# Gate projections with tokens on partitions, turned through DRAM, and a planner with another load rate and finer keys

## The chip, the cores and the metric

The kernel runs on one core of one Trainium2 chip. The metric is the device time of one execution in microseconds; the median of three timed executions stands for the kernel. Beside these there is one profiled execution, from which every row of the trace comes.

## What is computed

A diffusion backbone of two layers over 256 latent tokens and 256 context tokens, 2048 channels, all in float32. Layer 0 runs two head groups side by side: neighbourhood attention (16 heads) and a bidirectional state-space scan (SSD, 8 groups). Each of them is multiplied by a SiLU gate that is projected from the same normalised input. Layer 1 is a gated short convolution. Cut to what the change touches:

```python
p = h @ w_in                                  # 256 x 2048 @ 2048 x 14400
ya = neighbourhood_attention(q, k, v, kc, vc, rpb)
ya = ya * jax.nn.silu(cols(p, COL_GATE_A, NA_WIDTH, 0))          # gate G, 2048 columns
yb = gated_group_rmsnorm(y_ssd + d * lat[0], cols(p, COL_Z, SSD_WIDTH, 0), ssm_norm_g)   # gate Z, 2048 columns
out = jnp.concatenate([ya, yb], axis=-1) @ w_out
x = x + gate[:, None] * out
```

## The kernel before

**Products in three parts.** Every large product is done in a reduced float32 form that TensorE streams at full rate. A weight chunk of 128 x 1024 values (512 KB) is loaded into one of five `raw` buffers (nine in the first phase, when four tiles of later use serve too), rounded by ScalarE into `wH` (L458), and the remainder is taken by VectorE into `wL` (L465). The input is held the same way as `hH` and `hL`. A product is the sum of three: hH wH + hL wH + hH wL. There are three pairs of wH and wL, and a chunk's low part gives the raw buffer back, which lets the next load be issued on SyncE's queue (L428).

**Two ways to lay a product.** `mm_ws` (L690) holds 128 columns of the weight as the stationary operand and streams the tokens: for a weight of 512 columns it needs, for each block of 128 input channels, 4 column blocks x 3 products. With the 256 latent tokens alone each matmul streams 256 columns. The result has channels on partitions. `mm_act` (L680) holds 128 tokens as the stationary operand and streams up to 512 weight columns: 2 token blocks x 3 products. The result has tokens on partitions. `proj(nc_, kind, ps, nxt)` (L731) runs one projection over the 16 blocks of input channels; its `kind` is a number of tokens for `mm_ws` and "act" for `mm_act`. In layer 0, Q, K and V use "act"; the SSD inputs B, C and X and the gates G and Z use `mm_ws`, because what uses them wants channels on partitions.

**The turn through DRAM.** Q and K come out with tokens on partitions and are needed the other way round. `kq_gen` (L1007) stores each normalised block of 128 tokens with its columns in a mixed order into a DRAM tensor, fetches it back with four DMAs, one for each group of 32 partitions (`fetch`, L241, issued on GpSimd's queue) into the tile D (`d_take`, L1003: one buffer, guarded by the flag `dfree`), and finishes with VectorE transposes of 32 x 32 blocks (`blocks`, L248). The heads take the same D tile for their probabilities (L1137 to L1152).

**The gates before.** `silu2_gen` (L1054) waits until the gate tile is free (`ok`: for G the four heads of the step before are done, for Z the two groups before), then takes tanh of half the projection from PSUM (ScalarE, L1059) and multiplies (th + 1) by the projection (VectorE, L1061) straight into the gate tile `gt` or `sz`, two PSUM banks for each gate. The banks are held until then.

**What sets the order.** The order of every engine's instructions is written out by the Python code before the kernel runs. A list of tasks (generators) yields what it needs next: an engine, tiles that must be ready, PSUM banks. `Plan` keeps an estimated time for each engine and each piece of a tile; `may` (L296) lets a task's next step be written when the plan says that its inputs are ready at about the time TensorE is at. Weight products are written in a fixed sequence, and between them `pump` writes the steps that are due: splits (`splits_try`, L491), attention heads (`head_gen`, L1074), SSD groups (`group_gen`, L1418), turns, and the matrix-vector products of later layers' modulation (`gemv_gen`, L840; its accumulation on VectorE is L857). A load costs its bytes divided by `RATE` in the plan, one load after another, with 1000 ns ahead of and behind it; a DMA that touches DRAM scratch has 3000 ns more. `keys` says which pieces of a tile count as one: 128 columns of an SBUF tile. The engines themselves run in order and wait on semaphores that follow from the real overlaps of tiles, whatever the plan thought.

**The sequence.** The first phase, about 170 us, runs in eight steps of 256 input channels: the products of the modulation weights (`ada_gen`, L746, which gives each step's A0 and S0), the modulated input of the step, and the partial products of K, V, Q and B. Then come G(0), dt, C, X and Z(0), then Q, K, G, V and the SSD inputs of the next quarter with Z, and so on; in the last quarter V and G come after Z, just before the out-projection. The out-projection, layer 1's in-projection and its out-projection are all "act".

Of the kernel before, what the change touches and what calls it, by code (L numbers as in the profile page):

```python
# [10 lines left out]
AF = mybir.ActivationFunctionType  # L11
ALU = mybir.AluOpType
AX = mybir.AxisListType

D = 2048
KB = 16
EPS = 1e-6
COL_Q, COL_G, COL_Z, COL_K, COL_V, COL_X = 0, 2048, 4096, 6144, 8192, 10240
# [19 lines left out]
class Plan:  # L38


    NAMES = {"PE": "PE", "DVE": "DVE", "Activation": "ACT", "Pool": "POOL", "SP": "SP"}
    RATE = 270.0

    def __init__(self):
        self.t = dict.fromkeys(("PE", "DVE", "ACT", "POOL", "SP"), 0.0)
# [4 lines left out]
    def keys(self, ap):  # L50
        a, n = ap.ap, ap.tensor.name
        if type(ap.tensor).__name__ == "Tile" and not n.startswith("dram"):
            lo = ap.offset % a[0][0] if a[0][0] else ap.offset
            hi = lo + sum(abs(s) * (c - 1) for s, c in a[1:])
            return [(n, u) for u in range(lo // 128, hi // 128 + 1)]
        if n.startswith("in_") or n.startswith("out_"):
            return []
        hi = ap.offset + sum(abs(s) * (c - 1) for s, c in a)
        return [(n, u) for u in range(ap.offset // 256, hi // 256 + 1)]
# [38 lines left out]
    def add(self, b):  # L98
# [10 lines left out]
        if op == "DMACopy":  # L109
# [4 lines left out]
            if e == "SP":  # L114
                self.dma = max(self.dma, s + 1000) + n / self.RATE
                done = free = self.dma + 1000
            else:
                done = free = max(self.dma, s + 1000) + n / self.RATE + 1500
            if any(a.tensor.name.startswith("dram") for a in ins + outs):
# [52 lines left out]
def kernel(ctx: ExitStack, tc, x, cx, ada_w, ada_b, w_in, w_out, sc_in, sc_out, rpb, small, const,  # L172
# [8 lines left out]
    w_in, w_out, sc_in, sc_out = (Laid(w, n) for w, n in ((w_in, "w_in"), (w_out, "w_out"), (sc_in, "sc_in"), (sc_out, "sc_out")))  # L181
    V, S, G, T, DMA = nc.vector, nc.scalar, nc.gpsimd, nc.tensor, nc.sync
    DMA2 = nc.scalar
    plan = Plan()
    E = plan.add

    def st(shape, tag, dt=F32, name=None):
        return sb.tile(list(shape), dt, tag=tag, name=name or tag, bufs=1)
# [12 lines left out]
    def drt(shape, name):  # L201
        return dr.tile(list(shape), F32, name="dram_" + name)
# [3 lines left out]
    free_t = [st([128, 512], f"tmp{k}") for k in range(NTMP)]  # L206
    free_h = [st([128, 256], f"half{k}") for k in range(NHALF)]
    free_b = [pj.tile([128, 512], F32, tag=f"bank{k}", name=f"bank{k}", bufs=1) for k in range(8)]
# [4 lines left out]
    KT, QT, Vt, gt = st([128, 4, 512], "KT"), st([128, 4, 256], "QT"), st([128, 4, 512], "Vt"), st([128, 4, 256], "gt")  # L213
    sz, xtm, yi = st([128, 4, 256], "sz"), st([128, 2, 512], "xtm"), st([128, 4, 256], "yi")
# [26 lines left out]
    def fetch(dst, src):  # L241

        n = src.shape[0] // 32
        for b in range(4):
            E(G.dma_start(dst[32 * b:32 * b + 32].rearrange("p t (a x) -> p (t a) x", a=4),
                             bass.AP(tensor=src.tensor, offset=src.offset + 128 * b, ap=[[512, 32], [32 * 512, n], [1, 128]])))

    def blocks(o, i):  # L248

        E(V.transpose(o.rearrange("p k (a j) -> p a k j", a=4), i.rearrange("p (a k j) -> p a k j", a=4, k=4)))  # L250

    urgent, side, back = [], [], []
    got = set()
# [4 lines left out]
    def spawn(q, gen, tmps=0, halves=0):  # L258
        q.append(Task(gen, tmps, halves))
# [120 lines left out]
    def banks(n):  # L380
        force(lambda: len(free_b) >= n)
        return [take(free_b) for _ in range(n)]
# [4 lines left out]
    def give(pool, *bs):  # L387
        pool.extend(bs)

    W_ = lambda eng, *aps, nb=0: (eng, aps, nb)  # L390
    when = lambda f: ("if", f, 0)
# [321 lines left out]
    def chunk(kb0, kind, ps, first, last, lhs=None):  # L713

        H, Lo = use()
        nb = H.shape[1]
        for j in range(nb):
            kb = kb0 + j
            aH, aL = (hH[kb], hL[kb]) if lhs is None else lhs(kb)
            f, l = first and j == 0, last and j == nb - 1  # L720
            if kind == "act":
                mm_act(ps, aH, aL, H[:, j], Lo[:, j], f, l)
            elif kind == "both":
                mm_both(ps, aH, H[:, j], Lo[:, j], f, l)
            else:
                mm_ws(ps, aH, aL, H[:, j], Lo[:, j], kind, f, l)
        used()
# [3 lines left out]
    def proj(nc_, kind, ps, nxt, leave=False):  # L731
        nb = 1024 // nc_
        for kb in range(0, KB, nb):
            if kb + 2 * nb >= KB:
                reserve[0] = nxt
            chunk(kb, kind, ps, kb == 0, kb + nb >= KB)
            if leave:
                free_rows[0] = kb + nb
        reserve[0] = 0
# [258 lines left out]
    attn = [0]  # L998

    kqd = drt([4, 768, 512], "kqd")  # L1000
    dfree = [True]

    def d_take(name):  # L1003
        dfree[0] = False
        return st([128, 2, 512], "PT0", name=name)
# [40 lines left out]
    def v_gen(a, ps):  # L1046
# [4 lines left out]
            give(free_b, ps[t])  # L1051
        got.add(("V", a))

    def silu2_gen(key, a, ps, dst, ok):  # L1054
        yield when(lambda: ok())
        for b in range(2):
            yield W_("ACT", ps[b])
            th = tmp()
            E(S.activation(th, ps[b], AF.Tanh, scale=0.5))  # L1059
            yield W_("DVE", th)  # L1060
            E(V.scalar_tensor_tensor(out=dst[:, 2 * b:2 * b + 2, :].rearrange("p b c -> p (b c)"), in0=th, scalar=1.0,  # L1061
                                     in1=ps[b], op0=ALU.add, op1=ALU.mult))
            give(free_t, th)
            give(free_b, ps[b])
        got.add((key, a))

    b0 = rpbs[0, :, :]
# [6 lines left out]
    def head_gen(a, h):  # L1074
        hd = 4 * a + h
# [58 lines left out]
        yield W_("POOL", ptd[hd])  # L1134
        give(free_t, sps[0], sps[1])
        yield ("cap", 0, 0)
        yield when(lambda: dfree[0] and (hd == 0 or ("d", hd - 1) in got))  # L1137
        Dt = d_take(f"D{hd}")
        got.add(("d", hd))
        yield W_("POOL", ptd[hd])  # L1140
# [151 lines left out]
    ssd_done = [0]  # L1292
    Btm = [None]

    def make_b(s, ps):

        bts = []
        for i in range(2):
            bt, th = tmp(), tmp()
            b3, t3 = two(bt), two(th)  # L1300
            yield from conv(ps[i], 16 + 2 * s + i, 2, b3, t3)
            if i == 0:
                yield when(lambda: not (ssd_done[0] < 2 * s))
                yield W_("DVE", th)
            give(free_b, ps[i])
            conv_end(b3, t3, b3)
            give(free_t, th)
            bts.append(bt)
        for i in range(2):
            b3 = two(bts[i])  # L1310
            yield W_("PE", bts[i], nb=1)
            E(S.copy(Bl[:, i, :], b3[:, 0, :]))
            pt = bank()
            for t in range(2):
                turn(pt[:, t * 128:(t + 1) * 128], b3[:, 1, t * 128:(t + 1) * 128])
                turn(pt[:, 256 + t * 128:256 + (t + 1) * 128], b3[:, 0, t * 128:(t + 1) * 128])
            yield W_("ACT", pt)
            E(S.copy(Btm[0][:, i], four(pt)))
            give(free_b, pt)
            give(free_t, bts[i])  # L1320
        got.add(("B", s))

    def make_c(s, ps):
        yield when(lambda: not (ssd_done[0] < 2 * s))
        for i in range(2):
            ac, th = half(), half()
            c3, t3 = ac.rearrange("p (s t) -> p s t", s=1), th.rearrange("p (s t) -> p s t", s=1)
            yield from conv(ps[:, i * 256:(i + 1) * 256], 24 + 2 * s + i, 1, c3, t3)
            conv_end(c3, t3, Cl[:, i:i + 1, :])
            give(free_h, ac, th)  # L1330
        give(free_b, ps)
        got.add(("C", s))
# [191 lines left out]

    def do_g(a, nxt):
        psG = banks(2)
        proj(512, 256, psG, nxt)
        spawn(urgent, silu2_gen("G", a, psG, gt, lambda: attn[0] >= 8 * a and (a or ("K", 0) in got)), 1)

    def do_ssd(s, nxt):  # L1530
        if s:
            psB = banks(2)
            proj(256, 512, psB, 1)
            spawn(urgent, make_b(s, psB), 3)
        psC, = banks(1)
        proj(256, 256, [psC], 4)
        spawn(urgent, make_c(s, psC), 0, 2)
        psX = banks(4)
        proj(512, 512, psX, 2)
        for gi in range(2):  # L1540
            spawn(urgent, make_x(s, gi, psX[2 * gi:2 * gi + 2]), 3)
        psZ = banks(2)
        proj(512, 256, psZ, nxt)
        spawn(urgent, silu2_gen("Z", s, psZ, sz, lambda: ssd_done[0] >= 2 * s and ("K", 0) in got), 1)
        for gi in range(2):
            spawn(side, group_gen(s, gi), 3, 4)

# [2 lines left out]
    for h in range(4):  # L1550
        spawn(side, head_gen(0, h))
# [27 lines left out]
    for a in range(1, 3):  # L1579
        do_qk(a, 2)  # L1580
        do_gv(a, 2)
        do_ssd(a, 2)
# [235 lines left out]
    cg, u, v = st([128, 4, 256], "gt", name="cg"), st([128, 4, 256], "sz", name="u"), st([128, 4, 256], "QT", name="v")  # L1818
# [87 lines left out]
    for i in range(4):  # L1906
        pss = []
        for part in (1, 2, 0, 3):
            ps = banks(2)
# [94 lines left out]
```

## Time and profile before

| | |
|---|---|
| three timed runs | 1763.7, 1769.4, 1769.15 us; median 1769.15 |
| the profiled execution's own time | 1762.67 us |
| its span, first to last instruction | 1760.9 us |
| granted TensorE clock, mean | 0.999 |
| moved by DMA | 412.5 MB, 234 GB/s over the span |

The page names a tile by the program's name with its number left out: `wH` and `wL` are the two parts of a weight, `hH` and `hL` those of layer 0's input, `bank` is PSUM. A matmul row gives the streamed operand first and the stationary one after it, then the stationary shape and the streamed shape: `bank<-hH,wH 128*128 128x256` streams 256 tokens past a weight, `bank<-wH,hH 128*128 128x512` streams 512 weight columns past 128 tokens. Mean durations of matmuls overlap one another; the distance from one start to the next is the rate.

### The profile page before, as it was taken

To read this page: it belongs to the slowest core of one execution; us is meant where nothing else is said; L and a number is where in the kernel's file an instruction comes from. 1 tells how busy PE (TensorE), PEld (TensorE's weight loads), DVE (VectorE), ACT (ScalarE), POOL (GpSimd) and SP (SyncE) were. 2 spreads that over 40 slices of the span, in tenths; PEclk is the share of its full clock that TensorE was granted. 3 is DMA by queue.
4 is the path that set the end of the run, shared out by engine and by line. 5 is a ranking of instruction groups with operands and counts; after the bars stand their busy time and mean duration, and the time that the engine had idled before them with its cause. 6 is when DMAs were issued, how large, how long until landed. Compare 5 with 4: busy or idle time off the path is not lost.

```text
span 1760.9 us, 25272 instructions
## 1 busy us (share of the span) xinstructions
PE 1728.3 (98%) x9305; PEld 1442.4 (82%) x9305; DVE 1292.8 (73%) x2041; ACT 785.3 (45%) x1186; POOL 191.0 (11%) x300
## 2 busy tenths in 40 slices
PE   6999999999999999999999999999999999999998
PEld 4677988889888889888888898888878888888887
DVE  5566877888787987786888698876667776766555
ACT  5422335454354453353453444654435444444442
POOL 0000111013111012111012101110000000000000
PEclk9999999999999999999999999999999999999999
DMA  9987675577876677866577767787766888876774
GB/s 349 344 291 252 214 227 181 181 214 241 261 227 201 190 219 248 262 193 204 170 239 227 215 188 226 224 261 253 268 216 232 265 281 266 267 248 216 219 231 158
DMA packets 147629, 412.50 MB, mean 234 GB/s; under 512 B 34304, under 2 KB 48272, under 8 KB 147504
## 3 DMA queue, kind: packets, MB, share of 16 engines
q1 hardware_dynamic: 132112, 366.64, 64.0%
q0 software_dynamic: 15392, 44.24, 8.0%
q8 instruction: 73, 1.20, 0.3%
q14 instruction: 52, 0.43, 0.1%
HBM read 386.53 MB, written 25.59 MB: 234 GB/s over the span
## 4 chain that ended last, share of the span: by engine, by line
PE 94%; DVE 2%; DMA 1%; ACT 1%; issue 1%; SPq 0%; POOL 0%; DVEq 0%; ACTq 0%; POOLq 0%
PE bank L231 93%; PE bank L235 1%; DVE wL L465 1%; DMA raw<-in_ada_w 0%; ACT wH L458 0%; DMA half<-in_rows 0%; DVE hL L804 0%; SPq L618 0%; DMA raw<-in_sc_in 0%; DVE tmp L1283 0%; DVE h L1729 0%; DVE tmp L800 0%; ACT h L1748 0%; ACT hH L798 0%; DVE xm L664 0%
## 5 line engine op out<-in xcount | busy, mean ns | idle before, releaser
L458 ACT CAST wH<-raw 128x1024 fp32r<-128x1024 f32 (+1 forms) x440 | 459.5, 1045 | 664.0 <-PE bank L231 559.6
L465 DVE TENSOR_TENSOR wL<-raw,wH 128x1024 fp32r<-128x1024 f32 (+1 forms) x440 | 532.2, 1213 | 257.4 <-ACT wH L458 255.0
L231 PE MATMUL bank<-hH,wH 128*128 128x256 f32 (+1 forms) x1040 | 341.0, 328 | 0.9 <-ACT wH L458 0.9
L231 PE MATMUL bank<-hL,wH 128*128 128x256 f32 (+1 forms) x1040 | 337.0, 324 | 0.0
L231 PE MATMUL bank<-hH,wL 128*128 128x256 f32 (+1 forms) x1024 | 331.4, 324 | 3.1 <-DVE wL L465 3.1
L231 PE MATMUL bank<-wH,h 128*128 128x512 f32 x1024 | 316.8, 390 | 1.7 <-DVE h L1729 1.7
L231 PE MATMUL bank<-wH,hH 128*128 128x512 f32 x640 | 256.0, 400 | 4.8 <-ACT hH L798 2.6
L231 PE MATMUL bank<-wL,hH 128*128 128x512 f32 x640 | 249.9, 391 | 0.3 <-DVE wL L465 0.3
L231 PE MATMUL bank<-wH,hL 128*128 128x512 f32 x640 | 249.3, 390 | 0.1
L231 PEld LDWEIGHTS bank<-wH,h 128*128 128x128 f32 x1024 | 191.9, 188 | 43.5 <-DVE h L1729 3.0
L231 PEld LDWEIGHTS bank<-hH,wH 128*128 128x128 f32 x1040 | 197.8, 190 | 18.9 <-issue 2.0
L231 PEld LDWEIGHTS bank<-hL,wH 128*128 128x128 f32 x1040 | 197.8, 190 | 15.8
L231 PEld LDWEIGHTS bank<-hH,wL 128*128 128x128 f32 x1024 | 194.6, 190 | 19.4 <-DVE wL L465 4.1
L857 DVE SCALAR_TENSOR_TENSOR acc<-raw,csil,acc 128x512 f32<-128x512 f32 x240 | 179.1, 746 | 30.9 <-DMA raw<-in_ada_w 27.2
L231 PE MATMUL bank<-wL,h 128*128 128x512 f32 x512 | 199.4, 389 | 0.2 <-DVE wL L465 0.2
L231 PE MATMUL bank<-wH,mix 128*128 128x512 f32 x512 | 160.9, 391 | 0.0
L231 PEld LDWEIGHTS bank<-wH,hH 128*128 128x128 f32 x640 | 120.1, 188 | 36.3 <-issue 7.2
L231 PEld LDWEIGHTS bank<-wH,hL 128*128 128x128 f32 x640 | 120.1, 188 | 25.4 <-DVE hL L804 0.6
L231 PEld LDWEIGHTS bank<-wL,hH 128*128 128x128 f32 x640 | 120.1, 188 | 25.0 <-DVE wL L465 1.1
L231 PEld LDWEIGHTS bank<-wL,h 128*128 128x128 f32 x512 | 96.1, 188 | 20.6 <-DVE wL L465 0.6
L231 PEld LDWEIGHTS bank<-wH,mix 128*128 128x128 f32 x512 | 96.1, 188 | 20.4 <-issue 0.5
L231 PE MATMUL bank<-wL,mix 128*128 128x512 f32 x256 | 99.7, 390 | 0.0
(276 smaller groups left out, 1856.5 us busy)
## 6 DMA issues: line engine op xcount, KB each, us to landing
raw<-in_w_in SPq DMA_DIRECT2D x209, 512.0 KB
raw<-in_ada_w SPq DMA_DIRECT2D x163, 512.0 KB
raw<-in_sc_in SPq DMA_DIRECT2D x128, 512.0 KB
raw<-in_w_out SPq DMA_DIRECT2D x64, 512.0 KB
raw<-in_sc_out SPq DMA_DIRECT2D x32, 512.0 KB
dram_ptd<-tmp POOLq DMA_DIRECT2D x32, 256.0 KB, 4.9
D<-dram_ptd POOLq DMA_DIRECT2D x64, 128.0 KB, 5.6
tmp<-dram_csr SPq DMA_DIRECT2D x32, 256.0 KB
```

Of the source, the lines that this page charges most:

```text
L231: E(T.matmul(o, l, r, start=start, stop=stop, skip_group_check=True))
L235: E(T.transpose(o, i, ident if k == 128 else ident[:k, :k]))
L458: E(S.copy(H, v))
L465: E(V.tensor_tensor(out=Lo, in0=v, in1=H.bitcast(F32), op=ALU.subtract))
L857: E(V.scalar_tensor_tensor(out=acc, in0=v[:, j], scalar=csil[:, 2 * k + j:2 * k + j + 1], in1=acc, op0=ALU.mult, op1=ALU.add))
```

## The change

Both gates are projected with `kind` "act". `silu2_gen` now does the tanh and the multiply for each block of 128 tokens into a tmp tile, gives the PSUM bank back, stores the block into a DRAM tensor `gzd`, waits until the gate tile and the D tile are free, fetches both blocks into D and turns them into the gate tile with `blocks`. The task is counted with two tmp tiles instead of one. The columns of G and Z in the weight are put into the mixed order on the host, so that the projection comes out in the order that the store wants. A head takes the D tile for its probabilities only after its gate is there. In the planner a load counts 400 bytes a ns instead of 270, and `keys` makes pieces of 4 columns in tiles with less than 256 columns and of 2 columns in the tiles `small` and `const`, where pieces had 128 columns.

```diff
-    RATE = 270.0
+    RATE = 400.0
...
-            return [(n, u) for u in range(lo // 128, hi // 128 + 1)]
+            k = 4 if a[0][0] < 256 else 2 if n.startswith(("small", "const")) else 128
+            return [(n, u) for u in range(lo // k, hi // k + 1)]
...
+    gzd = drt([8, 256, 512], "gzd")
+
     def silu2_gen(key, a, ps, dst, ok):
-        yield when(lambda: ok())
-        for b in range(2):
-            yield W_("ACT", ps[b])
+        ths = []
+        src = gzd[4 * (key == "Z") + a]
+        for t in range(2):
+            yield W_("ACT", ps[t])
             th = tmp()
-            E(S.activation(th, ps[b], AF.Tanh, scale=0.5))
+            E(S.activation(th, ps[t], AF.Tanh, scale=0.5))
             yield W_("DVE", th)
-            E(V.scalar_tensor_tensor(out=dst[:, 2 * b:2 * b + 2, :].rearrange("p b c -> p (b c)"), in0=th, scalar=1.0,
-                                     in1=ps[b], op0=ALU.add, op1=ALU.mult))
-            give(free_t, th)
-            give(free_b, ps[b])
+            E(V.scalar_tensor_tensor(out=th, in0=th, scalar=1.0, in1=ps[t], op0=ALU.add, op1=ALU.mult))
+            give(free_b, ps[t])
+            yield W_("POOL", th)
+            E(G.dma_start(src[t * 128:(t + 1) * 128], th))
+            ths.append(th)
+        yield W_("POOL", src)
+        give(free_t, *ths)
+        yield ("cap", 0, 0)
+        yield when(ok)
+        yield when(lambda: dfree[0])
+        Dt = d_take(f"D{key}{a}")
+        yield W_("POOL", src)
+        fetch(Dt, src)
+        for t in range(2):
+            yield W_("DVE+", Dt)
+            blocks(dst[:, :, t * 128:(t + 1) * 128], Dt[:, t])
+        dfree[0] = True
         got.add((key, a))
...
-        yield when(lambda: dfree[0] and (hd == 0 or ("d", hd - 1) in got))
+        yield when(lambda: dfree[0] and ("G", a) in got and (hd == 0 or ("d", hd - 1) in got))
...
-        proj(512, 256, psG, nxt)
-        spawn(urgent, silu2_gen("G", a, psG, gt, lambda: attn[0] >= 8 * a and (a or ("K", 0) in got)), 1)
+        proj(512, "act", psG, nxt)
+        spawn(urgent, silu2_gen("G", a, psG, gt, lambda: attn[0] >= 8 * a and (a or ("K", 0) in got)), 2)
...
-        proj(512, 256, psZ, nxt)
-        spawn(urgent, silu2_gen("Z", s, psZ, sz, lambda: ssd_done[0] >= 2 * s and ("K", 0) in got), 1)
+        proj(512, "act", psZ, nxt)
+        spawn(urgent, silu2_gen("Z", s, psZ, sz, lambda: ssd_done[0] >= 2 * s and ("K", 0) in got), 2)
...
+    w_in = np.array(f('na_ssd_w_in')[0])
+    w_in[:, COL_G:COL_K] = w_in[:, COL_G:COL_K].reshape(D, 8, 4, 4, 32).transpose(0, 1, 3, 2, 4).reshape(D, 4096)
```

More of the change, by code (lines that the diff above doesn't have):

```diff
@@ L1987 @@
     arr = {
[L1988 removed]
+        'x': f('x')[0], 'cx': f('ctx')[0], 'ada_w': np.concatenate([laid(f('ada_w')[k], f'ada_{k}') for k in range(2)]), 'ada_b': f('ada_b'), 'w_in': laid(w_in, 'w_in'),
         'w_out': laid(f('na_ssd_w_out')[0], 'w_out'),
```

1 line of the change is left out of this document (removed).

## The prediction

> **What bounds the kernel now.** I read the page's busy time and its chain first, then what TensorE waits for, then its groups by shape, then the order of its matmuls in time.
>
> ```profile
> PE 1728.3 (98%) x9305; PEld 1442.4 (82%) x9305; DVE 1292.8 (73%) x2041; ACT 785.3 (45%) x1186; POOL 191.0 (11%) x300
> ...
> PE 94%; DVE 2%; DMA 1%; ACT 1%; issue 1%; SPq 0%; POOL 0%; DVEq 0%; ACTq 0%; POOLq 0%
> ...
> PE bank L231 <- DVE rx L606: 13.1, 1, 13.1
> PE bank L231 <- DVE wL L465: 3.6, 5, 2.3
> ```
>
> TensorE is busy for 98% of the 1760.9 us span and is 94% of the chain that ended last. Its longest wait, 13.1 us once, is the start (first input and its norm). The next, late low parts of split weights, is 3.6 us in all. So a step is worth what it changes in TensorE's own time, and work on another engine costs only what it makes TensorE wait. A busy share does not tell the rate, because one matmul's recorded duration overlaps the next; for the rate I take start to start.
>
> ```profile
> L231 PE MATMUL bank<-hH,wH 128*128 128x256 f32 x640 | 183.3, 286 | 0.0
> L231 PE MATMUL bank<-wH,hH 128*128 128x512 f32 x640 | 256.0, 400 | 4.8 <-ACT hH L798 2.6 <-DVE sz L830 1.5 <-DVE gt L830 0.8
> ...
> 200.95 0.28 PE L231 MATMUL bank<-hH,wH 128*128 128x256 f32 x1
> ...
> 223.86 0.28 PE L231 MATMUL bank<-hH,wL 128*128 128x256 f32 x1
> ...
> 438.75 0.39 PE L231 MATMUL bank<-wH,hH 128*128 128x512 f32 x1
> ...
> 446.91 0.39 PE L231 MATMUL bank<-wH,hH 128*128 128x512 f32 x1
> ```
>
> The form with the weight as stationary operand and 256 tokens streamed (names hH,wH) appears 640 times for each of the three products. Eight gate projections (four G, four Z) at 64 make 512 of these; the four C projections make the other 128. The rows at 200.95 and 223.86 are the first and last matmul of one whole gate projection, the 192 matmuls of G(0): 22.91 us over 191 steps, **119.9 ns** each. The last two rows are 36 matmuls apart in the K projection, which already has tokens as the stationary operand and streams 512 weight columns: 8.16 us, **226.7 ns** each. Two matmuls of 256 columns take 239.9 ns, one of 512 takes 226.7.
>
> **The change part by part.**
>
> *Gate matmuls.* Each gate projection goes from 192 matmuls of 256 columns (23.03 us) to 96 of 512 (21.76 us): 1.27 us less, and for eight **10.1 us** less, all on TensorE, in stretches where it never stands idle. The number of streamed columns stays; what goes is a fixed 13 ns or so for each of the 768 matmuls saved. Both rates come from this kernel in the same span, so I keep this term between 9 and 10.2; the lower end allows for matmuls slowed where attention's small products stand between them.
>
> The Trainium skill, "TensorE: Matmul & The Clock Gate", section "Back-to-back issue gap", gives a warm gap of N / 2.4 + 2.5 ns for an isolated matmul; the estimate by that page is 109.2 ns for 256 and 215.8 for 512, and the change would save 768 times 2.5 ns, 1.9 us. The two rates measured here, in a stream with a weight load for each matmul, say 13 ns, so the trace does not bear the page's fixed part out.
>
> *The way of the gate through DRAM.* The tanh (L1059) and the multiply (L1061) stay, the multiply now writing its tmp. Added for each gate: two stores, four fetches, two 32x32-block transposes, the same steps that Q takes today:
>
> ```profile
> L250 DVE STREAM_TRANSPOSE QT<-kqD_Q 128x512 f32<-128x512 f32 x8 | 5.2, 686 | 0.0
> L1059 ACT ACTIVATE tmp<-bank 128x512 f32<-128x512 f32 x16 | 9.0, 591 | 0.0
> ...
> L245 POOL DMA_DIRECT2D kqD_Q<-dram_kqd x16 | 9.4, 592 | 28.1 <-DVE PL L1151 10.9 <-DVE KT L250 9.1 <-issue 4.4
> ...
> L1029 POOL DMA_DIRECT2D dram_kqd<-tmp x24 | 13.4, 559 | 19.1 <-DVE tmp L1024 13.4 <-DMA tmp<-dram_csr 2.2 <-DVE tmp L1464 1.7
> dram_kqd<-tmp POOLq DMA_DIRECT2D x24, 256.0 KB, 4.7
> kqD_Q<-dram_kqd POOLq DMA_DIRECT2D x16, 128.0 KB, 4.8
> 300.00:400.00 100.00, 100.00 (x563) 85.05 (x562) 85.55 (x156) 51.47 (x94) 9.67 (x15) 1.00 0.67 193
> ```
>
> VectorE gains 16 x 0.686 = 11 us spread over eight places; in its fullest 100 us (the window row: TensorE, weight loads, VectorE 85.55) it still has 14 us free. POOL gains 16 x 0.559 + 32 x 0.592 = 28 us on 191, its queue 48 DMAs. Traffic grows by 8 x 1 MB on 412.5 MB, 2%. Behind a POOL wait stand attention's stores and fetches, and the stores of finished mixes; who waits for those are heads, not the weights. The cover is that TensorE has weights' products to do meanwhile; where heads are due at once, a late gate costs its delay one to one.
>
> The latency of a gate, its multiply counted like the transpose of the same shape, is the sum 0.6 + 0.7 + 4.7 + 4 x 0.59 + 4.8 + 2 x 0.69, about 14.5 us after its last matmul, plus a turn at the one D tile that K, Q and the heads use too. The edit at L1137 makes a head wait for its gate before it takes D, so the gate cannot be locked out. The tight place is the last one, because G(3) is projected just before V(3) and the out-projection:
>
> ```profile
> 1074.10 0.28 PE L231 MATMUL bank<-hH,wL 128*128 128x256 f32 x1
> ...
> 1127.25 0.28 PE L231 MATMUL bank<-PH,vH 128*128 128x256 f32 x1
> ...
> L231 PE MATMUL bank<-wH,mix x255: 387/389/504, 1120.7 to 1219.6; 128*128 128x512 f32 x128
> ...
> 1194.02 0.42 DVE L1170 SCALAR_TENSOR_TENSOR half<-bank,gt 128x256 f32<-128x256 f32 x1
> ```
>
> G(3)'s last matmul starts at 1074.1, head 12 first needs it at 1127.3: 53 us for 14.5 of gate and then about 12 for head 12's own fetch, turn and split. That is hidden, with 25 us to spare. After it each head follows the one before through V, as now. The last multiply by the gate is at 1194.0, and the out-projection's last two input pairs are due after 14 pairs x 24 matmuls x 0.2267 = 76 us from 1120.7 (the row with mix), about 1197 plus some 10 us of attention between. So heads that come over 10 us later would make TensorE wait. I take 0 for this part, bounds 0 to 8 (head 12 late by its whole spare). The gates' two PSUM banks come free at once instead of waiting for the last four heads (G) or groups (Z). TensorE is idle for 32.6 us in all, 13.1 of it the start, and no row names a bank as what it waited for, so the gain is between 0 and 3; I take 0.
>
> *The planner at 400 bytes a ns.* No instruction changes; a 512 KB load counts 1.31 us instead of 1.94. Work that uses a load is therefore written earlier into its engine's order and waits there if the load is late; what stands behind it waits too.
>
> ```profile
> 20.00:40.00 20.00, 16.35 (x104) 10.55 (x102) 12.71 (x36) 13.08 (x29) 1.59 (x4) 1.00 1.02 388
> 80.00:100.00 20.00, 18.53 (x130) 13.23 (x129) 11.61 (x22) 5.73 (x10) 0.00 (x0) 1.00 0.85 307
> 140.00:160.00 20.00, 20.00 (x137) 14.81 (x129) 12.41 (x22) 5.45 (x10) 0.00 (x0) 1.00 0.84 294
> ...
> DVE acc L857 <- DMA raw<-in_ada_w: 27.2, 14, 3.8
> ACT wH L458 <- issue: 69.8, 33, 6.0
> ACT wH L458 <- DMA raw<-in_w_in: 13.4, 6, 4.0
> ```
>
> With the DMA engines full (share 1.02) the loads ran at 388 GB/s, 1.35 us each; at a share of 0.85 they ran at 307. The old figure is below all of these rows, the new one above all. Already now VectorE and ScalarE stand 110 us in 53 waits that are or may be loads, yet TensorE's waits for split weights are 4.5 us with ScalarE's part, 4% of that, since three weight buffers lie between. If each of the 53 grows by 0.63 us, 33 us are added there and, at 4%, 1.4 us reach TensorE. The other side: in the rows at 20 and 80 TensorE is not full, 1.5 us idle in the second, and earlier entry of the ada products could win back some 3 us. Bounds -3 to +22 (the rival below); I take **+1.5**, nearest to the 4% row.
>
> The Trainium skill, "DMA: Bandwidth & Descriptors", section "Where 436 GB/s comes from", puts HBM's share of a core at about 358 GB/s; the row with 388 is above it. By the page a load takes 1.46 us, the plan would be early by 0.15 us a load, and the dear rival below would cost 8.4 us instead of 22.
>
> *Finer keys for small tiles.* The planner no longer holds the columns of one small tile (A0, statk, the constants) for one piece. Only the order written out changes, mostly in the first 170 us. Nothing in the trace prices it; the rows at 20 and 80 leave TensorE 3.65 and 1.47 us idle, so I bound it by -5 and +5 and take 0.
>
> *Sum.* -10.1 + 1.5 = -8.6 us. The profiled execution took 1762.67 us (span 1760.9 and 1.8 around it), so 1754.1 on its own scale. The three timed runs are 1763.7, 1769.15 and 1769.4, the profiled one is 6.5 below their median; the mean of all four is 1766.2, and from it the sum gives **1758**.
>
> **The rivals.**
>
> *Nothing to measure.* The gate arrives late where heads are due. D goes to K, Q, G and Z in turn; each use is 4 x 0.59 + 4.8 + 1.4, about 8.5 us. One more turn ahead of heads 12 to 15 uses up the 10 us of slack and, with POOL's queue, costs 4 to 9 us: 1766.2 - 10.1 + 4 to 9 = 1760 to 1765. For it: one D tile for all of them. Against it: 25 us to spare. The page's 2.5 ns a matmul ends here too: as a mechanism, saving one matmul saves only its issue, 1.9 us, 1764. So would a change that doesn't do what it says, where the 512-column form runs at 240 ns between attention's products; the rows deny both. Chance 0.20 together.
>
> *Slower: the plan runs ahead of the DMAs.* In the first eight steps TensorE takes ada weights in groups of four loads, two groups a step. If they are entered as landed at 1.31 us a load while 307 GB/s makes 1.71, each group stops TensorE for 4 x 0.40 = 1.6 us, and the 14 groups after the first step cost 22 us: 1766.2 - 10.1 + 22 = 1778. It decides from 0.72 us a group, where 14 groups eat the 10.1. For it: these loads go straight to TensorE with no split between, and the share is 0.84. Against it: nine load buffers are in use there, the engines have 15% left, and a load ahead of its use has landed whatever the plan thought. Chance 0.12.
>
> *More than the sum.* The waits of the first 100 us and of G(0)'s neighbours go too: -10.1 - 6, 1750. Chance 0.13.
>
> **How the numbers follow.** Forecast 0.55, more 0.13: faster by over 0.3% 0.68. Within 0.3% (5 us, about what a measurement of this kernel can tell from no change) 0.20; slower 0.12. The range goes from 1745, the rival of more with some 5 us for the runs' spread, to 1771, which takes in the late gate and half of the slower rival.
>
> **What would show it.** Right: the page counts 8537 matmuls, 768 fewer; the 128x256 form of hH,wH falls to 128 and the 128x512 form of wH,hH rises to 896, spaced 0.227; VectorE has 2057 instructions, POOL 348; TensorE's busy time is some 10 us less; and its waits for wL stay under 6 us. Wrong: TensorE waits for ada loads or wL in the first 170 us (the slower rival), for mixes at the out-projection near 1200 (the late gate), or the gates' 512-column matmuls are over 235 ns apart.

## The result, and the profile after

The changed kernel is slower: a median of 1816.7 us (six runs, 1807.7 to 1821.4) against 1768.5 for the kernel before (six runs), a ratio of 1.0273 [1.0245, 1.0300], 48 us more. The prediction was 1758 us, with 1745 to 1771 as its range and 0.12 for slower. The profiled execution took 1807.7 us, its span 1805.9.

The page of the changed kernel: busy time of each engine, the row of granted clock, the shares of the chain that ended last.

```profile
PE 1738.6 (96%) x8537; PEld 1405.7 (78%) x8537; DVE 1302.1 (72%) x2057; ACT 786.7 (44%) x1186; POOL 216.3 (12%) x348
...
PEclk9999999999999999999999998899999999999999
...
PE 61%; DMA 14%; DVE 11%; issue 3%; ACT 1%; POOL 1%; SPq 0%; DVEq 0%; ACTq 0%; POOLq 0%
```

Three things differ. TensorE has 768 matmuls fewer, as foretold, but its idle time went from 32.6 us (1760.9 - 1728.3) to 67.3 (1805.9 - 1738.6). It is busy for 10 us more, not 10 less, and two slices of the clock row are no longer 9: part of the matmuls took longer. And the chain of waits, 94% TensorE before, is now 61% TensorE, 14% DMA and 11% VectorE: the path to the end runs through loads, and through the engine that waits for them.

What TensorE waits for, first rows (us in total, times, longest):

```profile
PE bank L232 <- DMA raw<-in_ada_w: 15.5, 6, 13.3
PE bank L232 <- DVE wL L466: 9.0, 14, 3.0
PE bank L232 <- ACT Vt L1051: 7.6, 1, 7.6
PE bank L232 <- DVE tmp L1484: 6.8, 2, 4.3
```

The first row is mostly the start of the kernel (13.3 once; before, 13.1 for the first input). The others are late products of VectorE and ScalarE. The third, one wait of 7.6 us, is for PSUM banks that hold V of the last quarter, V(3): its last product starts at 1149.12 us, and ScalarE copies it out only at 1157.11, behind SSD steps, a weight cast and finished mixes in its order. This wait was 0.6 us in the kernel before. A reason for late products stands in the waits of the two engines themselves:

```profile
ACT wH L459 <- issue: 42.8, 19, 5.4
ACT wH L459 <- DMA raw<-in_w_in: 18.6, 9, 2.6
DVE acc L858 <- DMA raw<-in_ada_w: 74.3, 40, 8.7
```

VectorE's accumulation of the modulation (`gemv_gen`; L857 before, L858 after) waited 27.2 us in 14 waits, and now waits 74.3 in 40. VectorE takes its work in order, so during such a wait everything written behind it stands still. ScalarE's two rows ("issue" is idle time that the profile puts down to nothing) are 61 us together, 83 before, though the row put down to loads grew from 13.4 us in 6 waits to 18.6 in 9.

### The profile page after: what moved, and what is told of

The parts are those of the page before. It is cut to its first block, busy times and chain, and to the rows that moved or that the text cites. A ratio compares the mean times of both kernels' runs of the same rounds, so it can differ in the third digit from the quotient of the medians.

```text
span 1805.9 us, 23849 instructions
## 1 busy us (share of the span) xinstructions
PE 1738.6 (96%) x8537; PEld 1405.7 (78%) x8537; DVE 1302.1 (72%) x2057; ACT 786.7 (44%) x1186; POOL 216.3 (12%) x348
## 4 chain that ended last, share of the span: by engine, by line
PE 61%; DMA 14%; DVE 11%; issue 3%; ACT 1%; POOL 1%; SPq 0%; DVEq 0%; ACTq 0%; POOLq 0%
PE bank L232 61%; DMA raw<-in_ada_w 7%; DVE wL L466 3%; DVE acc L858 2%; DMA tmp<-dram_exr 1%; DMA tmp<-dram_csr 1%; DVE tmp L1300 1%; DMA kqD_K<-dram_kqd 1%; ACT wH L459 1%; DMA raw<-in_w_in 1%; DMA kqD_Q<-dram_kqd 1%; DMA D<-dram_ptd 1%; DMA bias<-dram_rpbs 1%; PE bank L236 1%; DMA raw<-in_sc_in 0%
## 5 line engine op out<-in xcount | busy, mean ns | idle before, releaser
L459 ACT CAST wH<-raw 128x1024 fp32r<-128x1024 f32 x439 | 459.1, 1047 | 665.2 <-PE bank L232 583.8
L466 DVE TENSOR_TENSOR wL<-raw,wH 128x1024 fp32r<-128x1024 f32 x439 | 530.7, 1215 | 220.3 <-ACT wH L459 218.8
L232 PE MATMUL bank<-wH,hH 128*128 128x512 f32 x896 | 360.0, 402 | 2.5 <-ACT hH L799 1.5
L232 PE MATMUL bank<-wL,hH 128*128 128x512 f32 x896 | 351.3, 392 | 1.2 <-DVE wL L466 1.2
L232 PE MATMUL bank<-wH,hL 128*128 128x512 f32 x896 | 350.7, 392 | 0.1
L858 DVE SCALAR_TENSOR_TENSOR acc<-raw,csil,acc 128x512 f32<-128x512 f32 x240 | 179.4, 747 | 77.9 <-DMA raw<-in_ada_w 74.3
L232 PE MATMUL bank<-hH,wH 128*128 128x512 f32 (+1 forms) x528 | 195.0, 369 | 0.0
L232 PE MATMUL bank<-hL,wH 128*128 128x512 f32 (+1 forms) x528 | 192.9, 365 | 0.0
L232 PE MATMUL bank<-hH,wL 128*128 128x512 f32 (+1 forms) x512 | 187.1, 365 | 4.3 <-DVE wL L466 4.3
L232 PEld LDWEIGHTS bank<-hH,wH 128*128 128x128 f32 x528 | 100.4, 190 | 16.7 <-issue 1.6
L232 PEld LDWEIGHTS bank<-hL,wH 128*128 128x128 f32 x528 | 100.5, 190 | 15.1
```

The costliest lines, as they stand in the source:

```text
L232: E(T.matmul(o, l, r, start=start, stop=stop, skip_group_check=True))
L459: E(S.copy(H, v))
L466: E(V.tensor_tensor(out=Lo, in0=v, in1=H.bitcast(F32), op=ALU.subtract))
L858: E(V.scalar_tensor_tensor(out=acc, in0=v[:, j], scalar=csil[:, 2 * k + j:2 * k + j + 1], in1=acc, op0=ALU.mult, op1=ALU.add))
```

## The experiments

**The theory** after the first comparison (A in the expectations below): the plan at 400 bytes a ns enters VectorE's modulation work before its loads have landed; VectorE waits in order; what stands behind is late for TensorE; and after such a gap the matmuls run at a lower clock. **Its rivals**: the gate's way through DRAM costs it, with heads late at the out-projection (B); or the finer keys (C); or any new order written out costs some, and no part of the change is the cause (D).

### Each part alone

The kernel before with one line changed (`rate_only`, `keys_only`), and the changed kernel with parts taken back (`gates_only`, `gates_keys`):

```diff
# gates_only: after with the old rate and the old keys; gates_keys: after with RATE = 270.0
# keys_only: before with the two new lines of keys; rate_only: before with
-    RATE = 270.0
+    RATE = 400.0
```

> The kernel before with loads counted at 400 bytes a ns and nothing else. Theory A: 1810 to 1830 us (the whole loss and the gates' 10 us, about 1768.5 + 58), VectorE waiting over 70 us for loads of ada weights. Theory B: 1768 us, no change. Theory C: 1768 us.

> The gates with tokens on partitions and through DRAM; loads counted at 270 bytes a ns and pieces of 128 columns, as before. Theory A (the loss is the planner's load rate, the gates save their 10 us): about 1758 us, TensorE's busy time some 10 us under the 1728.3 of before, clock 0.999. Theory B (the loss is the gates' own way through DRAM, one D tile and POOL's queue): over 1800 us, with waits at the out-projection's start as in the changed kernel. Theory C (the finer keys): about 1758 us, as A.

> The kernel before with the finer pieces of small tiles in the planner and nothing else. Theory A and theory B: 1768 us, within 5 us. Theory C: 1800 to 1830 us.

> The changed kernel with the load rate put back to 270 bytes a ns: gates and finer keys together. Theory A: about 1758 us. Theory B: over 1800 us. Theory C: over 1800 us. If gates and keys lose only together, this is over 1780 while each alone is under 1770.

| kernel | median us | to the kernel before | TensorE idle us | mean clock | VectorE's waits for modulation loads, us |
|---|---|---|---|---|---|
| before | 1767.3 | 1 | 32.6 | 0.999 | 27.2 |
| rate_only | 1826.8 | 1.0345 [1.0312, 1.0378] | 72.7 | 0.992 | 87.1 |
| keys_only | 1783.5 | 1.0092 [1.0066, 1.0118] | 42.6 | 0.996 | 40.5 |
| gates_only | 1776.9 | 1.0050 [1.0031, 1.0069] | 46.7 | 0.997 | 48.3 |
| gates_keys | 1779.7 | 1.0066 [1.0043, 1.0089] | 48.0 | 0.994 | 49.6 |
| after | 1816.7 | 1.0273 [1.0245, 1.0300] | 67.3 | 0.991 | 74.3 |

(The median of the kernel before is that of these runs; the last row was compared with 1768.5. Idle is span less busy time.) The rate alone costs 60 us, more than the whole change, and with the rate taken back (`gates_keys`) 12 are left of 48. No part alone is a gain: the gates, expected at 1758, took 1776.9, and the keys 16 us where at most 5 were expected. The parts do not add: 59.6 + 16.2 + 9.6 = 85 against 48; each writes out another order. But for `keys_only`, the last column rises with the time in these six kernels.

Where the time goes: the start of a stage's first weight matmul, found by counting the weight matmuls in the timeline of TensorE, us. The last row is the start of the out-projection's last product.

| stage starts | before | after | rate_only | keys_only | gates_only |
|---|---|---|---|---|---|
| G(0), end of the first phase | 200.9 | 205.3 | 208.3 | 209.5 | 201.7 |
| G(1) | 404.7 | 410.8 | 419.7 | 411.4 | 401.5 |
| B(1) | 476.8 | 496.4 | 508.4 | 483.0 | 479.3 |
| V(3) | 1074.2 | 1093.4 | 1124.0 | 1085.9 | 1079.2 |
| out-projection | 1120.7 | 1149.3 | 1171.8 | 1139.3 | 1127.7 |
| out-projection's end | 1309.2 | 1353.6 | 1370.0 | 1326.5 | 1322.2 |

Each column is one profiled execution. The kernel before took 1762.7 us in its own and 1767.3 in the median, so some 5 us in one row say nothing. In `rate_only` the first phase gives 7 of some 60 us; the rest comes in portions up to the end of the out-projection (8 up to G(1), 17 to B(1), 18 to V(3), 11 behind it), where the modulation of later layers is written between attention and the SSD. What follows adds almost nothing (453.7 us to the end, 451.7 before).

One such portion, in `rate_only`: B(1) starts at 508.4 instead of 476.8. Its timeline (start, duration, engine and operation, in brackets the idle time before it and what ended it) and TensorE in short stretches (busy, granted clock, DMA share, GB/s):

```profile
461.97 0.75 DVE L857 SCALAR_TENSOR_TENSOR acc<-raw,csil,acc 128x512 f32<-128x512 f32 x1 [4.57 <-DMA raw<-in_ada_w]
...
463.24 1.30 DVE L250 STREAM_TRANSPOSE QT<-kqD_Q 128x512 f32<-128x512 f32 x2
...
464.85 2.35 POOL L245 DMA_DIRECT2D kqD_K<-dram_kqd  x4 [12.88 <-DVE QT L250]
...
473.76 1.31 DVE L250 STREAM_TRANSPOSE KT<-kqD_K 128x512 f32<-128x512 f32 x2 [5.88 <-DMA kqD_K<-dram_kqd]
...
475.47 2.31 POOL L245 DMA_DIRECT2D kqD_K<-dram_kqd  x4 [8.27 <-DVE KT L250]
...
482.39 1.30 DVE L250 STREAM_TRANSPOSE KT<-kqD_K 128x512 f32<-128x512 f32 x2 [3.32 <-DMA kqD_K<-dram_kqd]
...
484.81 0.80 PE L231 MATMUL bank<-kH,qH 128*128 128x512 f32 x1 [9.36 <-ACT qH L1119]
...
486.55 0.63 PE L231 MATMUL bank<-wH,hH 128*128 128x512 f32 x1
...
486.97 0.63 PE L231 MATMUL bank<-wL,hH 128*128 128x512 f32 x1
```

```profile
484.00:486.00 2.00, 1.19 (x2) 0.50 0.00 0
486.00:488.00 2.00, 2.00 (x6) 0.50 0.13 29
488.00:490.00 2.00, 2.00 (x7) 0.59 0.93 352
490.00:492.00 2.00, 2.00 (x10) 1.00 0.36 147
```

From the top: VectorE waits 4.57 us for a modulation load. Q's turn stands behind it. POOL can fetch K into the same D tile only when Q is turned (12.88 us of waiting). K's turn waits for that fetch, the second fetch for that turn, the second turn for the second fetch, and TensorE, which needs K and Q, stands idle for 9.36 us. Up to 4.57 us of the 9.36 are VectorE's wait, handed on from step to step. The rest does not come from a later chain. In the kernel before, the chain runs at nearly the same times:

```profile
462.39 1.30 DVE L250 STREAM_TRANSPOSE QT<-kqD_Q 128x512 f32<-128x512 f32 x2
...
484.31 0.40 PE L231 MATMUL bank<-kH,qH 128*128 128x512 f32 x1
```

There TensorE does not wait, because the first product of K and Q stands behind 33 weight products of B(1) in its order. In `rate_only` it stands behind the 114th of V(1)'s 192, so 111 weight products earlier (some 25 us of TensorE's work at 0.227 each). The order written at 400 puts the heads earlier, and takes from TensorE the work that covered the chain. Two kernels of a later section divide this: with only the weights' loads at 400 the heads are early as well (147th of V(1)), with only the modulation's they are not (15th of B(1)).

The matmuls after the gap start 0.42 us apart instead of 0.227, at a granted clock of 0.50, and it is back at 490: some 5 us of work at half speed, 2 to 3 us more.

The same in the changed kernel, at 1105 to 1121 us, just before the out-projection:

```profile
1105.83 0.63 SPq L429 DMA_DIRECT2D raw<-in_ada_w  x1
...
1107.71 0.75 DVE L858 SCALAR_TENSOR_TENSOR acc<-raw,csil,acc 128x512 f32<-128x512 f32 x1
...
1109.34 0.76 DVE L981 TENSOR_TENSOR mix<-tmp,mix 128x256 fp32r<-128x256 f32 x2
...
1118.81 0.75 DVE L858 SCALAR_TENSOR_TENSOR acc<-raw,csil,acc 128x512 f32<-128x512 f32 x1 [8.71 <-DMA raw<-in_ada_w]
1119.48 0.61 DVE L1481 SCALAR_TENSOR_TENSOR tmp<-tmp,dtl,tmp 128x128 f32<-128x128 f32 x2
...
1120.60 0.69 PE L232 MATMUL bank<-tmp,xtm 128*64 128x128 f32 x2 [4.28 <-DVE tmp L1484]
```

```profile
1100.00:1120.00 20.00, 16.32 (x75) 0.96 0.89 269
1120.00:1140.00 20.00, 16.92 (x71) 0.79 0.57 168
1140.00:1160.00 20.00, 12.44 (x56) 0.81 0.76 232
```

The load is issued at 1105.83 and is there 13 us later; VectorE is through with its work at about 1110.1 and stands for 8.71 us. The SSD's two rows stand behind it, and TensorE gets the first of them 1.8 us after the load. In the 40 us from 1120 TensorE is busy for 29 and the clock is 0.8. Of the idle time there, 7.56 us are the wait for V(3)'s banks:

```profile
1157.74 1.19 PE L232 MATMUL bank<-tmp,xtm 128*64 128x128 f32 x8 [7.56 <-ACT Vt L1051]
```

`gates_only` has this wait at 4.5 us and `gates_keys` at 5.2, so it belongs to what the gates cost by themselves in these orders.

The Trainium skill, "TensorE: Matmul & The Clock Gate", section "Why this matters for your kernels", warns that gaps of more than about 3 us in TensorE's work cost the full clock. The traces agree for 9.36 and 4.28 us; shorter ones are in the last section.

### Moving the modulation's work later

If VectorE's early entry is the cause, entering it later should win the time back. `W_` with a "+" adds 1000 ns to what the plan holds of a load; the edit adds more for L857 alone:

```diff
-        late = eng[-1] == "+"
+        plus = eng.count("+")
...
-        rdy = plan.ready(aps) + (1000 if late else 0)
+        rdy = plan.ready(aps) + 1000 * plus
...
-                yield W_("DVE+", RAW["gem", n, k][1])
+                yield W_("DVE++++++", RAW["gem", n, k][1])    # margin6; "DVE++++" in margin4
```

> The kernel before with loads at 400 bytes a ns, but the accumulation of the modulation vector on VectorE (L857) is entered only when the plan has its load 6000 ns behind instead of 1000. Theory A2 (the loss comes through VectorE, which stands in order at L857 for loads of ada weights, 87 us in rate_only against 27 before): these waits fall under 30 us and the time to 1768 to 1780 us. Theory D (optimism harms everywhere, at the weight splits and the SSD rows too, or any new order is worse): over 1805 us although the waits fall.

> The changed kernel with the same margin of 6000 ns for L857's accumulation. Theory A2: 1756 to 1768 us, since the gates' 10 us then show. Theory D: over 1800 us.

> The gates alone (270 bytes a ns, coarse pieces) with a margin of 4000 ns for the accumulation. Theory A2: VectorE's waits for ada loads fall from 48 us to under 25 and the time from 1776.9 to 1755 to 1762. Theory B (the gates' way through DRAM itself costs 20 us): stays at 1770 to 1780.

> The kernel before with a margin of 4000 ns for the accumulation. Theory A2: the 27 us of waits fall towards 10 and the time by up to as much, 1750 to 1765. Theory D: 1768 or more, a new order being no better than the old.

All four missed: 1871.8, 1845.9, 1823.6 and 1831.4 us beside 1770.2, ratios 1.0589 [1.0566, 1.0612], 1.0433 [1.0415, 1.0450], 1.0310 [1.0293, 1.0326] and 1.0355 [1.0336, 1.0373]. TensorE's waits in the kernel before with margin 4, and POOL's store of the vector that layer 1 needs, in that kernel:

```profile
PE bank L231 <- DVE acc L857: 58.2, 3, 39.7
```

```profile
1369.03 0.57 POOL L869 DMA_DIRECT2D dram_mrow<-rowb  x1 [39.68 <-DVE rowb L866]
```

The margin slowed the whole chain of vectors, and the twelfth is stored at 1369 us, 1205 in the kernel before. The out-projection ends at 1303, so layer 1 waits for it. These totals therefore do not test the theory; the stages ahead do. `rate_margin6` reaches the out-projection at 1144.4 us and its end at 1334.1, `rate_only` at 1171.8 and 1370.0: 27 and 36 us won back by this one line.

The second try gives the margin to the first six vectors alone (`"DVE++++++" if n < 6 else "DVE+"`; four in `gates_margin4_half`), and takes a rate between the two:

> The kernel before with loads at 400 bytes a ns and a margin of 6000 ns for L857 in the first six of the sixteen vectors only, so that the twelfth is in time for layer 1. In rate_margin6 layer 1 began at 1334 against 1369 in rate_only, and lost 71 us afterwards to vectors that came late. Theory A2: the 35 us won ahead of layer 1 stay in part and the 71 go: 1790 to 1810 us against 1826.8. Theory D: 1820 or more.

> The changed kernel with the margin of 6000 ns in the first six vectors. Theory A2: 1775 to 1795 us against 1816.7. Theory D: 1810 or more.

> The gates alone with a margin of 4000 ns in the first six vectors. Theory A2: 1758 to 1768 us against 1776.9. Theory B (the way through DRAM itself): 1770 to 1780.

> The kernel before with loads counted at 330 bytes a ns. Theory A (optimism about loads costs in proportion): 1785 to 1805 us, between 1768 and 1827, VectorE's waits for ada loads between 27 and 87 us. Theory D (each new order is a lottery, the rate having no direction): anywhere, below 1775 or above 1815 as well.

| kernel | median us (1768.35 beside) | ratio | VectorE's waits for modulation loads, us | out-projection starts |
|---|---|---|---|---|
| rate_margin6_half | 1819.0 | 1.0285 [1.0262, 1.0309] | 76.3 | 1148.5 |
| changed_margin6_half | 1803.3 | 1.0200 [1.0171, 1.0229] | 61.0 | 1147.2 |
| gates_margin4_half | 1768.3 | 0.9997 [0.9985, 1.0009] | 16.5 | 1116.2 |
| rate330 | 1809.5 | 1.0234 [1.0217, 1.0252] | 82.0 | 1160.4 |

With the rate at 400 the line wins 8 and 13 us only. `rate_margin6_half` is 23 us ahead of `rate_only` at the out-projection and gives 15 of them back behind it (376.0 us from the last product of the out-projection to the first of layer 1's own out-projection, 360.9 in `rate_only`). With the gates alone it wins 8.5 us, all that they had cost. A rate of 330 already costs 41 us. The theory stands in direction, but this one entry does not hold the whole cost of the rate.

### Which loads

Only the modulation's loads counted at 400 (`rate_ada`), or only the weight chunks (`rate_weights`), the rest at 270; and, for the rival of the late gate, the gates alone with G(3) and Z(3) projected right after K(3) and their loads in that order (`gates_early`; a second kernel adds the margin of 4 in the first six vectors):

```diff
-                self.dma = max(self.dma, s + 1000) + n / self.RATE
+                self.dma = max(self.dma, s + 1000) + n / (400.0 if any(a.tensor.name == "in_ada_w" for a in ins) else self.RATE)
```

```diff
+    def do_z(s, nxt): ...            # Z's two lines of do_ssd; called first in do_ssd(3)
...
-        do_g(a, 4)
+        if a < 3:
+            do_g(a, 4)
...
+    do_g(3, 2)                       # right behind do_qk(3, 2)
```

> The kernel before with only the loads of modulation weights (in_ada_w) counted at 400 bytes a ns, all others at 270. Theory E (the plan believes these loads landed, and VectorE stands at L857): 1800 to 1827 us, VectorE's waits for them over 60 us. Theory F (the loss comes with the other loads, the weight chunks, and what stands behind them on SyncE's queue): 1768 to 1785 us.

> The kernel before with only the weight chunks of w_in, w_out, sc_in and sc_out counted at 400 bytes a ns, the modulation weights and the rest at 270. Theory E: 1768 to 1785 us. Theory F: 1800 to 1827 us. If both are high, the one shared clock of loads in the plan carries it, whichever load is counted low.

> The gates alone, and in the last quarter G(3) and Z(3) projected right after K, ahead of B, C, X and V, so that the turned gates are there before the out-projection. Theory G (what the gates lose is the late turn in the last quarter, 8.3 us in the out-projection of gates_only): 1764 to 1772 us against 1776.9. Theory D (any new order costs 10 to 20 us of fresh waits): 1775 or more.

> As gates_early, with the margin of 4000 ns for L857 in the first six vectors. Theories A2 and G together: 1756 to 1763 us against 1768.3 of gates_margin4_half. Theory D: 1768 or more.

Beside 1770.0: `rate_ada` 1817.0, 1.0260 [1.0241, 1.0280]; `rate_weights` 1780.9, 1.0062 [1.0047, 1.0077]. VectorE's waits for modulation loads are 78.1 and 63.8 us, TensorE's idle time 64.9 and 44.6. So 47 of the 60 us come from counting the modulation's loads early, 9 of them in the first phase (G(0) starts at 209.6), and 11 from the weights'; here the two nearly add up. The plan keeps one clock for all loads, so each edit moves the other loads in it too. `rate_weights` shows also that the length of VectorE's waits is no price: it has 64 us of them and costs 11. What counts is what stands behind.

`gates_early` came out as the rival D said: 1798.8, 1.0157 [1.0131, 1.0183], and with the margin 1786.8, 1.0099 [1.0081, 1.0117]. It reaches the out-projection at 1114.0, 13.7 us ahead of `gates_only`, but then the out-projection lasts 231 us from its first product to its last, instead of 195. X(3) now comes 49 us later, the last two SSD groups start at 1176 us instead of 1085, and TensorE waits for heads beside them:

```profile
1213.76 0.58 PE L231 MATMUL bank<-PH,vH 128*128 128x256 f32 x1 [9.63 <-ACT vH L1173]
```

### Is 270 a middle?

> The kernel before with loads counted at 230 bytes a ns. Theory A (optimism about loads costs, in one direction): at or below 1768 us, VectorE's waits for ada loads under 27 us. Theory D (270 is merely a good draw and every other figure draws a worse order): 1778 us or more.

> The gates alone (coarse pieces) with loads counted at 230 bytes a ns. Theory A: waits for ada loads from 48 towards 27 us or less, 1757 to 1768 us against 1776.9 of gates_only. Theory D: 1775 or more.

`rate230` (the kernel before with `RATE = 230.0`) takes 1783.7 beside 1770.2, 1.0075 [1.0052, 1.0097]. VectorE's waits for modulation loads fall to 11.4 us, and yet it is 13 us slower: the first phase ends 14 us later (G(0) starts at 214.8, 200.9 before), and the out-projection starts 17 us later, so little is won or lost in between. The gates with 230 take 1815.8, 1.0260 [1.0236, 1.0283]: G(0) 15 us late, and 32 us from the out-projection's last product to layer 1's first, 5.8 before, because the vector that layer 1 needs is stored at 1353 us. So the figure is dear on both sides: too low, and loads that are there are used late; too high, and VectorE stands before loads that are not. Both runs came out as the rival D said and not as A did. D is not excluded as a part of the cost: of the nineteen other orders timed here, the changed kernel's among them, every one but `gates_margin4_half` is 9 us or more behind the kernel before. The 60 us of the rate are more than any order at 270 costs without a longer margin (at most 29, `gates_early`).

## Why the prediction was wrong

**What bounds the kernel** was read rightly for the kernel before, TensorE at 98%. The inference that work on another engine costs only what it makes TensorE wait holds for most of the cost: of the 63 us that `rate_only`'s profiled execution is longer, 40 are idle time of TensorE, and 23 are longer busy time. What it missed is that this bound rests on the order written out, in which TensorE has weight products ahead of the heads and SSD steps that are not ready.

**Gate matmuls: right in the rate, not seen as a whole.** The groups by shape and the first and last row of G(0) in the changed kernel's timeline:

```profile
L232 PE MATMUL bank<-wH,hH 128*128 128x512 f32 x896 | 360.0, 402 | 2.5 <-ACT hH L799 1.5 <-DVE gt L831 1.0
...
205.30 0.39 PE L232 MATMUL bank<-wH,hH 128*128 128x512 f32 x1
...
226.83 0.39 PE L232 MATMUL bank<-wH,hL 128*128 128x512 f32 x1
```

G(0)'s 96 matmuls take 95 steps in 21.53 us, 0.2266 each, as foretold (0.2267). Its stage is 21.8 us from its start to that of dt, 23.0 before, the 1.27 us foretold for one gate. The eight together do not show: TensorE is busy for 1728.4 us in `gates_only` and for 1728.3 in the kernel before, and `gates_margin4_half` reaches G(3) 2.4 us ahead (1037.9, 1040.3 before) with seven gates behind it. What took the rest was not separated.

**The gate's way through DRAM: its latency wrong in size.** The latency of a gate was put at 14.5 us. G(3) in `gates_only`, rows of POOL, then of VectorE:

```profile
1083.96 0.57 POOL L1067 DMA_DIRECT2D dram_gzd<-tmp  x1 [20.37 <-DVE tmp L1064]
...
1086.03 0.57 POOL L1067 DMA_DIRECT2D dram_gzd<-tmp  x1 [0.66 <-DVE tmp L1064]
...
1093.41 2.34 POOL L245 DMA_DIRECT2D DG<-dram_gzd  x4 [3.47 <-DMA dram_gzd<-tmp]
```

```profile
1109.16 1.30 DVE L250 STREAM_TRANSPOSE gt<-DG 128x512 f32<-128x512 f32 x2
```

V(3) starts at 1079.2, the turns end at 1110.5: 31 us. The fetch is issued 6.8 us after the second store, and the turns come 13.4 us after the four fetches were issued, where the two transfers were put at 4.7 and 4.8 us: the sum of durations left out the queue and VectorE's place in line. Still inside the 53 us that the part had. Alone, the gates cost 9.6 us where -10.1 was forecast. The prediction found no row that names a bank; there is one, 0.6 us for V's banks, and with the gates it is 4.5. With the margin on L857 it is gone, and the out-projection starts 4.5 us ahead of the kernel before. That is given back after: TensorE waits for an SSD row, the clock falls, the out-projection ends 1.6 us later than before, and layer 1's first product follows 11.4 us after that instead of 5.8.

```profile
1124.44 0.85 PE L231 MATMUL bank<-tmp,xtm 128*64 128x128 f32 x5 [4.32 <-DVE tmp L1483]
```

```profile
1120.00:1140.00 20.00, 15.68 (x73) 12.88 (x72) 16.08 (x31) 11.64 (x24) 2.11 (x3) 0.91 0.72 239
```

**The planner at 400 bytes a ns: the step that failed.** The sum took +1.5 us, by "at 4%, 1.4 us reach TensorE" of 33 us that the waits would grow. Measured alone it is +60, so the term was too small by a factor of 40. Both of its factors were wrong. VectorE's waits for modulation loads did not grow by 0.63 us a wait (14 times that is 9 us) but by 60, from 14 waits to 44, since far more uses were written ahead of their loads; that the plan's lead adds up over a run of loads on one queue is the likely reason, and was not measured by itself. And the 4% was a share taken where three weight buffers cover; the work behind L857 (turns of K and Q, SSD rows, splits) has no such cover, and in the portion shown the new order also put the heads earlier among TensorE's products. TensorE's idle time grew by 40 us and its busy time by 23, of which the lowered clock is at most 13 ((0.999 - 0.992) x 1823.7); the rest is not split.

**The rival "the plan runs ahead of the DMAs"** named this mechanism and gave it 0.12, at 1778 us. Its place was wrong: it looked at the first eight steps, where TensorE itself takes the loads; there the rate cost 7 us, start and first phase together. The price came after, from loads that go through VectorE.

**Finer keys: 0, bounds -5 to +5; measured +16 alone**, 9 us of it by G(0). "Only the order written out changes" was right, and was no reason for a small bound. **The signs**: the counts of matmuls, VectorE and POOL instructions and the spacing came out as said; TensorE's busy time (10 us more) and its waits for wL (9.0, not under 6) did not.

**What stays open.** The line L857 accounts for 36 of the 61 us up to the end of the out-projection (`rate_margin6`); the rest, among it the weights' 11 us and the heads' earlier place, was not separated. How much of a new order's cost is mere chance (D) is open too. Why the changed kernel loses less than `rate_only` is not known beyond that its order is another one. No kernel tried is faster than the kernel before; `gates_margin4_half` equals it. A rate for the first phase and another behind it was not tried.

## What to carry to other kernels

In a kernel with a planned order, a figure of the planner is no cost of its own but a bet on every in-order engine: before raising an assumed DMA rate, list what stands behind each wait for a load on each engine, and take the cover of that work, not an average share. A gap on TensorE can cost some 2 us more after it, since the matmuls behind it run at half clock: here that followed every gap of over 2.8 us but two at the kernel's start, and a part of the shorter ones. A local saving of 10 us is worth having only with the order around it held fast, so measure it with the order's other causes taken out first.

## What the runs showed of the hardware

The clock falls after shorter gaps than the 3 us named above. In `gates_only` one of 2.67 us was enough; the timeline of TensorE, and its stretches of 2 us:

```profile
724.73 0.51 PE L231 MATMUL bank<-kH,qH 128*128 128x512 f32 x1 [2.67 <-ACT qH L1135]
```

```profile
724.00:726.00 2.00, 1.07 (x3) 0.92 0.91 311
726.00:728.00 2.00, 2.00 (x7) 0.50 0.79 213
728.00:730.00 2.00, 2.00 (x8) 0.72 0.90 231
```

The clock goes to 0.50 a microsecond after work has begun again, and stays there for some 3 us. In the changed kernel a gap of 2.53 us (421.11) was followed by 0.51, with three shorter ones some 6 us ahead of it, and one of 2.28 us (272.56) by no change.

```profile
421.11 0.66 PE L232 MATMUL bank<-tmp,xtm 128*64 128x128 f32 x8 [2.53 <-DVE half L1187]
```

```profile
422.00:424.00 2.00, 2.00 (x6) 0.51 0.21 36
```

```profile
272.56 0.63 PE L232 MATMUL bank<-half,half 128*128 128x32 f32 x4 [2.28 <-DMA half<-in_strict]
```

```profile
274.00:276.00 2.00, 2.00 (x11) 1.00 0.70 244
```

The length of one gap is not the whole rule. In `rate_only` one of 1.81 us was enough, and one of 2.79 us was followed by a clock of 1.00:

```profile
427.67 0.36 PE L231 MATMUL bank<-PH,vH 128*128 128x256 f32 x1 [1.81 <-DVE half L1512]
```

```profile
428.00:430.00 2.00, 2.00 (x13) 0.55 0.87 286
```

```profile
265.78 0.50 PE L231 MATMUL bank<-hH,wL 128*128 128x512 f32 x1 [2.79 <-DVE wL L465]
```

```profile
266.00:268.00 2.00, 2.00 (x10) 1.00 0.56 201
```

In the changed kernel three gaps of 1.41, 0.34 and 0.22 us close together (those before 413.77, 414.50 and 415.10) were followed by 0.50 too. In the twenty traces together, 47 of the 49 gaps of over 2.8 us were followed by the lower clock within 4 us (the other two at 14 and 15 us, `gates_rate230` and `rate230`), and 35 of the 79 between 1.5 and 2.8 us. What else decides is not known from these runs.
